# VectorE and ScalarE keep the written order of far-apart instructions in the RWKV recurrence of a hybrid DiT on one core

## The chip, the core and the metric

One core of a Trainium2 chip runs the whole forward pass in one launch. The metric is the device time of one execution in microseconds (us).

## The reference

The computation is a four-layer diffusion transformer on 256 latent and 256 context tokens, 1024 wide, in float32. The layers' mixers are, in this order, grouped-query attention with axial positions, neighbourhood attention on a 4 x 64 grid, a bidirectional RWKV-7 recurrence, and grouped-query attention again. Each layer adds a squared-ReLU MLP with 4096 hidden columns. The change lies in the third layer, whose core in the reference is a scan over tokens, run in both directions, for 16 heads of 64 columns:

```python
def step(s, inp):
    r_t, w_t, k_t, v_t, a_t, b_t = inp
    sa = jnp.einsum('nbhij,nbhj->nbhi', s, a_t)
    s = s * w_t[..., None, :] + sa[..., None] * b_t[..., None, :] + v_t[..., None] * k_t[..., None, :]
    return s, (jnp.einsum('nbhij,nbhj->nbhi', s, r_t) if emit else None)
```

## The kernel before

**Products.** Every weight is loaded in pieces of 128 x 1024 (`wr`) and split in two: ScalarE writes the high part `wh`, VectorE the remainder `wl` (class `Stream`, L259). A product is three TensorE matmuls: `wh`, `wl`, `wh` (L430 to L432; L470 to L472, tile `vps`, for the values of the RWKV layer, whose results are copied to `rV` at L1079, by VectorE and ScalarE in turn).

**The recurrence.** It is computed for pairs of heads, c = 0 to 7, each in blocks of 64 tokens. For one pair there are four kinds of work:
- `prep(c)` (L1099): gate products `wps` on TensorE with sigmoids `sg` and `ag` on ScalarE; the normed key (`ksq` on ScalarE, its sum over a head `kss` on TensorE, logarithm and exponential on ScalarE, `nkk`); the decays (a scan and `cc` on VectorE, two exponentials on ScalarE); the products `AR` and `BK`; a triangle `TT` from `tps`; a small triangular solve on GpSimd between two DRAM round trips, which ends in the load of `S` (L1234).
- `inverses(c)` (L1239): the transpose `R` of `S` on VectorE (L1250), `pa` and `pb` on TensorE with `cw` and `M` on VectorE, then `xd` on VectorE and four copies `Xt<-M` on ScalarE, `pv` and `px` on TensorE.
- `core(c)`, the chain (L1311): eight steps n, one after the other. A step's `zps` (TensorE) is copied to `z` (ScalarE), `ups` (TensorE) to `u` (ScalarE), then `sps` (TensorE) is scaled to the state `s` (VectorE), which the next step's `zps` needs. Masked products `nps` to `nmo` (VectorE), transposes `bkt` (copied by ScalarE) and the outputs `yps` stand beside it. 
- `post(c)` (L1414): group norm and gate of the outputs (`gm`, `bo`, `vT`, `gv`).

**What sets the order.** All these pieces are put in one list `todo` of (place, function). The place is counted in pairs: the chain of pair c has the places c to c + 1 in 46 or so equal steps, its `inverses` c - .65 to c - .1, its `prep` c - 2.4 to c - .9, its `post` c + 1 to c + 1.6. The list is sorted and the functions are called in that order (L1520); this is "the written order". It is not the order in which an engine executes: at build time a scheduler chooses, for each engine, among the instructions that are ready by its own cost model. It is bound by data and by order edges between two instructions of one engine, which set the order but give no semaphore. The class `InOrder` (L170) wraps an engine and can add such edges; before, it wraps ScalarE alone and is used only between `hold(True)` and `hold(False)`, outside the recurrence. An instruction that waits holds up those behind it in its engine's list, as the trace shows it where VectorE waits for `S`. Since ScalarE's calls pass through `InOrder`, all of its instructions have the line L180.

Of the kernel before, what the change touches and what calls it, by code (L numbers as in the profile page):

```python
# [169 lines left out]
class InOrder:  # L170


    def __init__(self, tc, engine):
        self.tc, self.engine, self.held, self.last = tc, engine, False, None

    def __getattr__(self, name):
        f = getattr(self.engine, name)

        def call(*args, **kw):
            x = f(*args, **kw)  # L180
            if self.held and getattr(x, "ins", None) is not None:
                if self.last is not None:
                    self.tc.add_manual_dep(x.ins, self.last, mybir.DependencyInfo(
                        mybir.DependencyClass.NoSync, mybir.DependencyReason.DATA), reason="order")
                self.last = x.ins.name
            return x
        return call

    def hold(self, on):
        self.held, self.last = on, None  # L190


@with_exitstack
def dit_kernel(ctx: ExitStack, tc: tile.TileContext, places, t_in, out, layers=DEPTH):
    nc = tc.nc
    pe, dve, pool, sp = nc.tensor, nc.vector, nc.gpsimd, nc.sync
    act = InOrder(tc, nc.scalar)

    one = ctx.enter_context(tc.tile_pool(name="one", bufs=1))
    k4p = ctx.enter_context(tc.tile_pool(name="k4", bufs=36))  # L200
# [11 lines left out]
    def pair(name, dt=F32):  # L212
        return k4(name, dt).rearrange("p (a t) -> p a t", a=2)

    def tmp(n, name):
        return t2p.tile([128, 520], F32, tag="t2", name=name)[:, 0:n]
# [4 lines left out]
    def bank(p, n, name):  # L221
        return p.tile([128, 512], F32, tag="b", name=name)[:, 0:n]
# [14 lines left out]
    def C(name, which="one"):  # L237
        o, shape = places[which][name]
        v = cs[which][:, o:o + int(np.prod(shape))]
        if len(shape) == 2:  # L240
            v = v.rearrange("p (a b) -> p a b", a=shape[0])
        elif len(shape) == 3:
            v = v.rearrange("p (a b c) -> p a b c", a=shape[0], b=shape[1])
        return v
# [178 lines left out]
    def split(dst, src, a, b, eng=dve):  # L423
        act.copy(out=dst[:, 0, a:b], in_=src)
        eng.tensor_tensor(out=dst[:, 1, a:b], in0=src, in1=dst[:, 0, a:b].bitcast(F32), op=ALU.subtract)  # L425
# [108 lines left out]
    def affine(dst, src, ca, cb, eng=None):  # L534
        (eng or dve).tensor_scalar(out=dst, in0=src, scalar1=ca, scalar2=cb, op0=ALU.mult, op1=ALU.add)
# [384 lines left out]
    def rwkv(i, hx, gate, nrm, begun, ends):  # L920
# [11 lines left out]
        def behind(x, others):  # L932
            for y in others:
                tc.add_manual_dep(x.ins, y.ins.name, mybir.DependencyInfo(
                    mybir.DependencyClass.NoSync, mybir.DependencyReason.DATA), reason="table set")

        def log(**kw):
            x = act.activation(**kw)
            if tables["set"] is not None:
                behind(x, [tables["set"]])  # L940
            tables["logs"].append(x)
# [113 lines left out]
        def keys(c):  # L1055
            def go():
                if c == 9:
                    W.depth = 1
                keep(c, 1, gemm(W.next("rw_wk", 0, "T", 0, c), m, ALL))
                if c == 7:  # L1060
                    made[4](PM)
            return go
# [351 lines left out]
        def post(c):  # L1414
            q = st[c]
            hold = {}

            def mean():
                y = tmp(512, "y")
                act.copy(out=y, in_=q["y"])  # L1420
                ps = bank(ps_s, 512, "gm")
                pe.matmul(ps, lhsT=ones64, rhs=y, start=True, stop=True)
                dve.scalar_tensor_tensor(out=y, in0=ps, scalar=-1.0 / 64, in1=y, op0=ALU.mult, op1=ALU.add)
                sq = tmp(512, "ysq")
                act.activation(out=sq, in_=y, func=AF.Square)
                hold["y"], hold["sq"] = y, sq

            def bonus():
                ps = bank(ps_s, 512, "bo")
                pe.matmul(ps, lhsT=ones64, rhs=q["rkd"], start=True, stop=True)  # L1430
                bo = q["rkd"]
                act.copy(out=bo, in_=ps)
                pt = bank(ps_s, 512, "vT")
                for blk in range(8):
                    for e in range(2):
                        pe.matmul(pt[half[e], blk * 64:blk * 64 + 64], lhsT=V[blk // 2][half[e], blk % 2, c], rhs=ident[half[e], half[e]], start=True, stop=True)
                dve.tensor_tensor(out=bo, in0=pt, in1=bo, op=ALU.mult)
                hold["bo"] = bo

            def var():  # L1440
                ps = bank(ps_s, 512, "gv")
                pe.matmul(ps, lhsT=ones64, rhs=hold["sq"], start=True, stop=True)
                r = hold["sq"]
                log(out=r, in_=ps, func=AF.Ln, bias=epg, scale=1.0 / 64)
                log(out=r, in_=r, func=AF.Exp, scale=-0.5)

            def normed():
                y = hold["y"]
                dve.tensor_tensor(out=y, in0=y, in1=hold["sq"], op=ALU.mult)
                affine(y, y, C("lnx_g", "rw")[:, c:c + 1], C("lnx_b", "rw")[:, c:c + 1])  # L1450

            def gated():
                ps = bank(ps_s, 512, "g")
                g2 = sml.tile([128, 128], F32, tag="g2", bufs=1, name="g2")
                sp.dma_start(out=g2, in_=t_in["rws"][c, :, 2])
                pe.matmul(ps, lhsT=g2, rhs=sig, start=True, stop=True)
                y = hold["y"]
                dve.tensor_tensor(out=y, in0=y, in1=hold["bo"], op=ALU.add)
                dve.tensor_tensor(out=y, in0=y, in1=ps, op=ALU.mult)

            def parts():
                o[c] = pair("o", F32R)
                split(o[c], hold["y"], 0, 512)
            return [mean, bonus, var, normed, gated, parts]
# [5 lines left out]
        def over(todo, a, b):  # L1470

            n = len(todo)
            return [(a + max(b - a, 0) * x / max(n - 1, 1), f) for x, f in enumerate(todo)]

        def weave(main, *side):

            for _, f in sorted(over(main, 0, 1) + [p for x in side for p in x], key=lambda p: p[0]):
                f()
# [19 lines left out]
        todo = over([keys(c) for c in range(8)], -2.6, -1.5)  # L1498
# [18 lines left out]
            todo += over([step(k) for k in range(9)], c - 2.4, c - 1.5)  # L1517
            todo += over([step(k) for k in range(9, 13)], c - 1.4, c - .9)
        todo.append((7., last_weights))
        for _, f in sorted(todo, key=lambda p: p[0]):  # L1520
            f()
        weave(begins, over(post(7), 0, .9))
        state["x"] = [pair("x") for _ in range(4)]
        for j in range(4):
# [127 lines left out]
    for i in range(layers):  # L1652
# [10 lines left out]
        def mid():  # L1663
            mod_to(i, 5)
            cols["e"] = Ends(nrm, i, 0, scales(i, 1, ln(0)))
            return cols["e"]

        streams = (gqa, natten, rwkv)[i % 3](i, get_h, gate, nrm, begun, mid)
        begun = cols["e"]
        nrm2 = Norm()  # L1670
# [37 lines left out]
def build(arrays, places, **kw):  # L1708
    import concourse.bacc as bacc

    nc = bacc.Bacc("TRN2", target_bir_lowering=False, num_devices=1)
    t_in = {n: nc.dram_tensor(f"in_{n}_dram", a.shape, F32, kind="ExternalInput").ap() for n, a in arrays.items()}
    out = nc.dram_tensor("out_0_dram", (128, 8, 256), F32, kind="ExternalOutput").ap()
    with tile.TileContext(nc) as tc:
        dit_kernel(tc, places, t_in, out, **kw)
    return nc
# [10 lines left out]
```

## Time and profile before

| | us |
|---|---|
| three runs | 2596.41, 2596.42, 2589.53 (median 2596.41) |
| the profiled execution, its own time | 2597.49 |
| its span, first to last instruction | 2595.7 |
| TensorE (PE) busy in it | 2469.1 (95%) |
| VectorE (DVE) busy | 1670.3 (64%) |
| ScalarE (ACT) busy | 1183.6 (46%) |
| GpSimd (POOL) busy | 267.7 (10%) |

The recurrence lies between about 1400 and 1850 us of the span. A row of the timeline gives start, duration, engine, line, operation, output and inputs, shapes and count, and in brackets how long the engine was idle before it and what ended that. A row of the waits gives the instruction that waited, what it waited for, the total in us, the number of times and the longest. A row of the windows gives the stretch, its length, the busy time of each engine, the clock that TensorE was granted as a share of its full 2.4 GHz, and the load of the DMA engines.

### The profile page before, as it was taken

The numbers are of one execution on the slowest core, as the hardware profiler recorded it, in microseconds if no ns is written. First come the engines' busy times: TensorE is split into PE (matmuls) and PEld (weight loads), VectorE is DVE, ScalarE is ACT, GpSimd is POOL, SyncE is SP. The second block draws the span as 40 slices with busy tenths as digits, with TensorE's granted clock in tenths as the row PEclk, the third lists the DMA queues.
The fourth block names the chain that finished last, engine by engine and source line by source line (L and its number), as shares of the span: only waits on it lengthen the run. The fifth ranks groups of instructions, "written<-read, shape, count | busy, mean of one in ns | idle before, by whom it ended". The sixth has DMA issues, their size and how long they took to land. (4 is left out here: it accounts for less than half of the span.)

```text
span 2595.7 us, 53219 instructions
## 1 busy us (share of the span) xinstructions
PE 2469.1 (95%) x22353; PEld 2096.9 (81%) x22353; DVE 1670.3 (64%) x3055; ACT 1183.6 (46%) x2214; POOL 267.7 (10%) x406
## 2 busy tenths in 40 slices
PE   8999999999999999999789799899989999999998
PEld 5778888889767888888767677778888888888997
DVE  3557677775566767787776565663658663766554
ACT  3555433244566543234455444544362343465644
POOL 0003000002000300000302112111030000221000
PEclk9999999999999999999899899999999999999998
DMA  8532556642111245664122311210336654223562
GB/s 324 170 124 66 180 192 191 208 147 94 59 60 58 82 144 182 202 210 162 67 95 83 78 28 32 41 23 12 140 95 215 208 188 126 82 66 106 179 188 89
DMA packets 158416, 324.14 MB, mean 125 GB/s; under 512 B 77392, under 2 KB 80992, under 8 KB 158176
## 3 DMA queue, kind: packets, MB, share of 16 engines
q1 hardware_dynamic: 158176, 320.73, 39.1%
q8 instruction: 176, 2.88, 0.5%
q14 instruction: 64, 0.52, 0.1%
HBM read 310.71 MB, written 9.97 MB: 124 GB/s over the span
## 5 line engine op out<-in xcount | busy, mean ns | idle before, releaser
L430 PE MATMUL mm<-h,wh 128*128 128x512 f32 (+1 forms) x1472 | 515.8, 353 | 19.1 <-ACT wh L180 10.4
L432 PE MATMUL mm<-h,wl 128*128 128x512 f32 (+1 forms) x1472 | 514.5, 350 | 4.3 <-DVE wl L280 4.0
L431 PE MATMUL mm<-h,wh 128*128 128x512 f32 (+1 forms) x1472 | 513.3, 349 | 2.6 <-DVE h L425 2.5
L180 ACT CAST wh<-wr 128x1024 fp32r<-128x1024 f32 x363 | 373.7, 1049 | 272.1 <-DVE wl L280 96.7
L280 DVE TENSOR_TENSOR wl<-wr,wh 128x1024 fp32r<-128x1024 f32 x340 | 426.5, 1261 | 93.6 <-ACT wh L180 72.0
L430 PE MATMUL mm<-f,wh 128*128 128x512 f32 (+1 forms) x1168 | 397.9, 341 | 0.0
L431 PE MATMUL mm<-f,wh 128*128 128x512 f32 (+1 forms) x1168 | 396.8, 340 | 0.0
L432 PE MATMUL mm<-f,wl 128*128 128x512 f32 (+1 forms) x1168 | 396.7, 340 | 0.0
L430 PEld LDWEIGHTS mm<-h,wh 128*128 128x128 f32 x1472 | 281.2, 192 | 63.9 <-ACT wh L180 12.5
L432 PEld LDWEIGHTS mm<-h,wl 128*128 128x128 f32 x1472 | 282.3, 192 | 42.7 <-DVE wl L280 6.9
L431 PEld LDWEIGHTS mm<-h,wh 128*128 128x128 f32 x1472 | 282.4, 192 | 39.3 <-DVE h L425 5.4
L431 PEld LDWEIGHTS mm<-f,wh 128*128 128x128 f32 x1168 | 221.6, 190 | 24.7
L430 PEld LDWEIGHTS mm<-f,wh 128*128 128x128 f32 x1168 | 221.6, 190 | 24.5
L432 PEld LDWEIGHTS mm<-f,wl 128*128 128x128 f32 x1168 | 221.6, 190 | 24.1
L180 ACT ACTIVATE relu<-mm 128x512 f32<-128x512 f32 (+1 forms) x146 | 72.5, 497 | 368.1 <-PE mm L432 368.1
L425 DVE TENSOR_TENSOR f<-sqr,f 128x512 fp32r<-128x512 f32 (+1 forms) x146 | 87.3, 601 | 229.4 <-ACT f L180 229.1
L483 DVE SCALAR_TENSOR_TENSOR x<-mm,gate,x 128x256 f32<-128x256 f32 x280 | 127.1, 480 | 142.8 <-PE mm L432 142.5
L280 POOL TENSOR_TENSOR wl<-wr,wh 128x1024 fp32r<-128x1024 f32 x23 | 60.8, 2645 | 1407.9 <-ACT wh L180 1400.4
L387 DVE SCALAR_TENSOR_TENSOR mwt<-mwt,srow 128x1024 f32<-128x1024 f32 x144 | 175.8, 1221 | 9.4 <-DMA mwt<-in_mwr_dram 8.0
L387 DVE SCALAR_TENSOR_TENSOR mpr<-mwt,srow 128x1024 f32<-128x1024 f32 x112 | 136.7, 1221 | 0.5
L430 PE MATMUL mm<-o,wh 128*128 128x256 f32 (+1 forms) x400 | 120.7, 303 | 0.3 <-ACT o L180 0.2
L432 PE MATMUL mm<-o,wl 128*128 128x256 f32 (+1 forms) x400 | 119.4, 299 | 0.3 <-DVE wl L280 0.2
(275 smaller groups left out, 4416.9 us busy)
## 6 DMA issues: line engine op xcount, KB each, us to landing
wr<-in_gw_dram SPq DMA_DIRECT2D x363, 512.0 KB, 3.7
mwt<-in_mwr_dram SPq DMA_DIRECT2D x144, 512.0 KB, 4.3
mwt<-in_mw_dram SPq DMA_DIRECT2D x48, 512.0 KB, 5.6
srow<-srow_d SPq DMA_DIRECT2D x6, 512.0 KB, 3.9
nab<-in_nab_dram SPq DMA_DIRECT2D x8, 384.0 KB, 3.3
rk<-rk_d SPq DMA_DIRECT2D x6, 512.0 KB, 4.7
rk_d<-rkp SPq DMA_DIRECT2D x10, 256.0 KB, 2.1
x<-in_xt_dram SPq DMA_DIRECT2D x4, 512.0 KB, 10.2
```

Of the source, the lines that this page charges most:

```text
L180: x = f(*args, **kw)
L280: self.lo[self.done % len(self.lo)].tensor_tensor(out=lo, in0=t, in1=hi.bitcast(F32), op=ALU.subtract)
L387: dve.scalar_tensor_tensor(out=to, in0=t, scalar=1.0, in1=rw_["s"][cnd], op0=ALU.mult, op1=ALU.mult, accum_out=m[:, cnd, r * 8 + c:r * 8 + ...
L425: eng.tensor_tensor(out=dst[:, 1, a:b], in0=src, in1=dst[:, 0, a:b].bitcast(F32), op=ALU.subtract)
L430: pe.matmul(ps, lhsT=st, rhs=hl[:, 0, a:b], start=first, stop=False)
L431: pe.matmul(ps, lhsT=st, rhs=hl[:, 1, a:b], start=False, stop=False)
L432: pe.matmul(ps, lhsT=wl[:, c * 128:(c + 1) * 128], rhs=hl[:, 0, a:b], start=False, stop=last)
L483: dve.scalar_tensor_tensor(out=xc(c)[:, a:b], in0=ps[:, a - base:b - base], scalar=gate[:, cnd, c:c + 1], in1=xc(c)[:, a:b], op0=ALU.mult, ...
```

## The change

`InOrder` gets a second mode, `within(reach)`, and VectorE is wrapped too. While the sorted list of the recurrence is called, each new instruction of VectorE or ScalarE gets an order edge to every earlier one of its engine whose place is lower by 0.1 or more (edges to instructions more than 0.3 back follow through those between). Two instructions of one engine that lie 0.1 of a pair apart can thus no longer be swapped by the scheduler; closer ones can. No instruction, transfer or buffer is added or taken away.

```diff
--- before.py
+++ after.py
@@ -170,31 +170,47 @@
 class InOrder:
 
 
+
     def __init__(self, tc, engine):
         self.tc, self.engine, self.held, self.last = tc, engine, False, None
+        self.reach, self.place, self.past = None, 0.0, []
+
+    def behind(self, x, name):
+        self.tc.add_manual_dep(x.ins, name, mybir.DependencyInfo(
+            mybir.DependencyClass.NoSync, mybir.DependencyReason.DATA), reason="order")
 
     def __getattr__(self, name):
         f = getattr(self.engine, name)
 
         def call(*args, **kw):
             x = f(*args, **kw)
-            if self.held and getattr(x, "ins", None) is not None:
+            if getattr(x, "ins", None) is None:
+                return x
+            if self.held:
                 if self.last is not None:
-                    self.tc.add_manual_dep(x.ins, self.last, mybir.DependencyInfo(
-                        mybir.DependencyClass.NoSync, mybir.DependencyReason.DATA), reason="order")
+                    self.behind(x, self.last)
                 self.last = x.ins.name
+            elif self.reach is not None:
+                for p, y in self.past:
+                    if p <= self.place - self.reach:
+                        self.behind(x, y)
+                self.past = [(p, y) for p, y in self.past if p > self.place - 3 * self.reach]
+                self.past.append((self.place, x.ins.name))
             return x
         return call
 
     def hold(self, on):
         self.held, self.last = on, None
+
+    def within(self, reach):
+        self.reach, self.past = reach, []
 
 
 @with_exitstack
 def dit_kernel(ctx: ExitStack, tc: tile.TileContext, places, t_in, out, layers=DEPTH):
     nc = tc.nc
-    pe, dve, pool, sp = nc.tensor, nc.vector, nc.gpsimd, nc.sync
-    act = InOrder(tc, nc.scalar)
+    pe, pool, sp = nc.tensor, nc.gpsimd, nc.sync
+    act, dve = InOrder(tc, nc.scalar), InOrder(tc, nc.vector)
 
     one = ctx.enter_context(tc.tile_pool(name="one", bufs=1))
     k4p = ctx.enter_context(tc.tile_pool(name="k4", bufs=36))
@@ -1517,8 +1533,14 @@
             todo += over([step(k) for k in range(9)], c - 2.4, c - 1.5)
             todo += over([step(k) for k in range(9, 13)], c - 1.4, c - .9)
         todo.append((7., last_weights))
-        for _, f in sorted(todo, key=lambda p: p[0]):
+
+        for eng in (act, dve):
+            eng.within(0.1)
+        for place, f in sorted(todo, key=lambda p: p[0]):
+            act.place = dve.place = place
             f()
+        for eng in (act, dve):
+            eng.within(None)
         weave(begins, over(post(7), 0, .9))
         state["x"] = [pair("x") for _ in range(4)]
         for j in range(4):
```

TensorE, GpSimd and SyncE get no edges of their own, but the scheduler's choices for them follow. In the row lists that the two kernels give, 208 of VectorE's 2801 instructions stand elsewhere, 104 of ScalarE's 2104, 686 of TensorE's 16807, 5 of SyncE's 735 and none of GpSimd's; all lie in the recurrence. In the changed kernel VectorE's instructions have the helper's line L186 too.

Three places. The first is ScalarE in the second half of a pair's chain, beside the `inverses` of the next pair (`Xt`, `v1`) and the start of the `prep` of the third one on (`sg`, `ag`, `ksq`); the same pattern stands in five pairs, c = 0 to 4. `z_15209`, `u_15227` and `bkt_15266` are the chain's copies. Before:

```order
L180 COPY z_15209<-zps_15200 128x128
L180 COPY u_15227<-ups_15222 128x128
L180 COPY bkt_15266<-bkt_15257 128x256
L180 ACT_TABLE_LOAD
L180 ACTIVATE sg_15142<-wps_15140,cs_rw_11519 128x8x64
L180 ACTIVATE sg_15146<-wps_15144,cs_rw_11519 128x8x64
L180 ACTIVATE ag_15150<-wps_15148,cs_rw_11519 128x512
L180 ACTIVATE ag_15153<-wps_15151,cs_rw_11519 128x512
L180 ACT_TABLE_LOAD
L180 COPY Xt_12313<-M_15065 32x16x32 x4
L180 ACTIVATE ksq_15229<-rk_14605,cs_rw_11519 128x512
```

And now:

```order
L186 COPY z_15209<-zps_15200 128x128
L186 ACT_TABLE_LOAD
L186 ACTIVATE sg_15142<-wps_15140,cs_rw_11519 128x8x64
L186 ACTIVATE sg_15146<-wps_15144,cs_rw_11519 128x8x64
L186 ACTIVATE ag_15150<-wps_15148,cs_rw_11519 128x512
L186 ACTIVATE ag_15153<-wps_15151,cs_rw_11519 128x512
L186 ACT_TABLE_LOAD
L186 COPY Xt_12313<-M_15065 32x16x32 x4
L186 COPY u_15227<-ups_15222 128x128
L186 ACTIVATE ksq_15229<-rk_14605,cs_rw_11519 128x512
L186 COPY v1_15238<-pv1_15239 128x128
L186 COPY bkt_15266<-bkt_15257 128x256
```

The chain's `u` stood ahead of the sigmoids and the copies `Xt<-M`; now it stands behind them, and the chain's `bkt` behind `ksq` and `v1`.

The second is VectorE at the start of the recurrence, around the transpose `R` of pair 0 (`S` comes by a DMA, `rV` are the value copies, `wl` the weights' remainders). Before:

```order
L1143 TENSOR_TENSOR cc_12877<-sg_12749 128x520
L1143 TENSOR_TENSOR cc_12941<-sg_12753 128x520
L1079 COPY rV_12766<-vps_12795 64x128 x2
L1250 STREAM_TRANSPOSE R_13055<-S_12738 128x512
L1079 COPY rV_12767<-vps_12795 64x128 x2
L1173 TENSOR_TENSOR fcol_13384<-sg_12749,cc_12877 128x3
L1173 TENSOR_TENSOR fcol_13384<-sg_12749,cc_12877 128x1
L1173 TENSOR_TENSOR fcol_13384<-sg_12749,cc_12877 128x3
L1173 TENSOR_TENSOR fcol_13384<-sg_12753,cc_12941 128x7
L1079 COPY rV_12768<-vps_12881 64x128 x2
L1079 COPY rV_12769<-vps_12881 64x128 x2
```

And now, the rows that end with the same transpose (`ag_12395` is of pair 0's `prep`, `AR`, `BK` and `TT` of pair 1's):

```order
L186 TENSOR_TENSOR ag_12395<-ag_12395,ag_12398 128x512
L186 TENSOR_TENSOR wl_12959<-wr_12800,wh_12958 128x1024
L186 SCALAR_TENSOR_TENSOR ag_12395<-ag_12395,cs_rw_11519,rk_11585 128x512
L186 TENSOR_TENSOR wl_12989<-wr_12830,wh_12988 128x1024
L186 TENSOR_TENSOR AR_13026<-nkk_12871,sg_12753 128x8x64
L186 COPY rV_12766<-vps_12957 64x128 x2
L186 COPY rV_12767<-vps_12957 64x128 x2
L186 SCALAR_TENSOR_TENSOR BK_13027<-nkk_12871,ag_12760 128x512
L186 TENSOR_TENSOR BK_13027<-BK_13027,cc_12941 128x512
L186 TENSOR_TENSOR TT_13032<-tps_13033,cs_rw_11519 128x512
L186 STREAM_TRANSPOSE R_13055<-S_12738 128x512
L186 COPY rV_12768<-vps_13057 64x128 x2
```

The transpose stood behind the first two `rV` copies and ahead of the others; now it comes some 25 instructions later, behind both `cc`, the products `AR` and `BK`, two `wl` and a `TT`.

The third is VectorE at the start of pair 0's chain, whose first `nmo` is `nmo_13571`. Before:

```order
L1079 COPY rV_12768<-vps_13469 64x128 x2
L1079 COPY rV_12769<-vps_13469 64x128 x2
L1332 TENSOR_TENSOR nmo_13571<-nps_13572,cs_rw_11519 128x384
L1275 TENSOR_TENSOR M_13280<-pb_13247,S_12738 128x256
L1275 TENSOR_TENSOR M_13280<-pb_13349,R_13055 128x256
L1119 MEMSET sg_13392 128x8
```

And now:

```order
L186 TENSOR_SCALAR ksq_13415<-kss_13417 128x512
L186 TENSOR_TENSOR BK_12946<-ag_12757,cc_12877 128x512
L186 SCALAR_TENSOR_TENSOR nkk_13422<-rk_12955,nkk_c_11525,ksq_13415 128x512
L186 SCALAR_TENSOR_TENSOR sg_13392<-resets_12306,sg_13392 128x520
L186 COPY rV_12768<-vps_13469 64x128
L186 TENSOR_TENSOR cc_13465<-sg_13392 128x520
L186 COPY rV_12768<-vps_13469 64x128
L186 COPY rV_12769<-vps_13469 64x128 x2
L186 TENSOR_TENSOR AR_13026<-rk_11638,sg_12753 128x8x64
L186 TENSOR_TENSOR fcol_13384<-sg_12753,cc_12941 128x7
L186 SCALAR_TENSOR_TENSOR sg_13396<-resets_12306,sg_13396 128x520
L186 TENSOR_TENSOR nmo_13571<-nps_13572,cs_rw_11519 128x384
```

The chain's `nmo` stood ahead of both `M`; now pair 1's `ksq`, `nkk`, its scans and `cc` and the last value copies are ahead of it.

## Rows read from the trace of the kernel before

**Rows 1.** The page: busy time of the engines, and the group of the high-part casts.

```profile
PE 2469.1 (95%) x22353; PEld 2096.9 (81%) x22353; DVE 1670.3 (64%) x3055; ACT 1183.6 (46%) x2214; POOL 267.7 (10%) x406
...
L180 ACT CAST wh<-wr 128x1024 fp32r<-128x1024 f32 x363 | 373.7, 1049 | 272.1 <-DVE wl L280 96.7
```

**Rows 2.** The windows from one pair's kss to the next; the clock is the column after POOL.

```profile
1579.93:1626.49 46.56, 42.54 (x1218) 34.48 (x1218) 29.86 (x63) 24.23 (x55) 10.49 (x32) 1.00 0.21 37
1626.49:1674.59 48.10, 43.71 (x1219) 35.11 (x1219) 29.89 (x63) 24.25 (x56) 10.41 (x32) 0.96 0.19 34
1674.59:1721.26 46.67, 42.69 (x1218) 34.56 (x1218) 29.98 (x63) 24.23 (x55) 10.78 (x34) 1.00 0.18 33
```

**Rows 3.** TensorE's waits from 1525 to 1750 us, five pairs: total, times, longest.

```profile
PE kss L1129 <- ACT ksq L180: 6.8, 5, 1.5
...
PE pv L1294 <- DVE xd L1281: 2.4, 5, 1.2
PE ups L1363 <- ACT z L180: 2.4, 5, 0.5
...
PE nps L1329 <- DVE nmo L1332: 1.6, 4, 0.5
PE zps L1355 <- DVE s L1384: 1.2, 5, 0.3
```

**Rows 4.** The timeline of ScalarE from 1568 to 1585 us, in one pair.

```profile
1569.11 0.27 ACT L180 COPY z<-zps 128x128 f32<-128x128 f32 x1 [1.26 <-PE zps L1355]
1570.01 0.27 ACT L180 COPY u<-ups 128x128 f32<-128x128 f32 x1 [0.64 <-PE ups L1363]
...
1571.62 1.28 ACT L180 ACT_TABLE_LOAD   x1
1572.91 1.26 ACT L180 ACTIVATE sg<-wps,cs_rw 128x512 f32<-128x512 f32 x2
...
1576.63 2.50 ACT L180 COPY Xt<-M 32x512 f32<-32x512 f32 x4
```

**Rows 5.** The timeline of TensorE in the same pair.

```profile
1569.51 0.40 PE L1363 MATMUL ups<-z,Xt 64*64 64x64 f32 x8
...
1572.25 1.13 PE L1114 MATMUL wps<-lora,wa 64*128 64x512 f32 x4
...
1576.38 0.45 PE L1374 MATMUL sps<-rV,bkt 64*64 64x64 f32 x8
1576.66 0.40 PE L1377 MATMUL sps<-u,bkt 64*64 64x64 f32 x8
```

**Rows 6.** All waits from 1425 to 1445 us, where the first pair's R is made.

```profile
DVE R L1250 <- DMA S<-rr: 8.3, 1, 8.3
...
PE pa L1259 <- DVE R L1250: 4.4, 1, 4.4
...
PE vps L470 <- ACT wh L180: 3.7, 1, 3.7
```

**Rows 7.** SyncE's queue from 1428 us, and the tile wr's issue-to-landing time.

```profile
1431.75 1.74 SPq L270 DMA_DIRECT2D wr<-in_gw_dram  x2
...
DMA to landing us min/median/max: 4.8/4.9/6.4
```

**Rows 8.** The timeline of VectorE from 1440 and from 1475 us.

```profile
1440.13 2.36 DVE L280 TENSOR_TENSOR wl<-wr,wh 128x1024 fp32r<-128x1024 f32 x2
...
1475.30 2.43 DVE L1140 TENSOR_TENSOR_SCAN sg<-resets,sg 128x520 f32<-128x520 f32 x2
...
1487.89 0.75 DVE L1134 SCALAR_TENSOR_TENSOR nkk<-rk,nkk_c,ksq 128x512 f32<-128x512 f32 x1 [1.91 <-ACT ksq L180]
```

**Rows 9.** TensorE from 1472 us, and short windows with the granted clock.

```profile
1472.71 0.33 PE L1329 MATMUL nps<-AR,BK 64*64 64x64 f32 x4 [2.47 <-ACT rV L180]
...
1473.00:1476.00 3.00, 2.34 (x36) 1.82 (x34) 1.96 (x6) 2.22 (x3) 2.52 (x7) 0.52 0.02 5
...
1626.70:1630.00 3.30, 3.30 (x32) 1.80 (x33) 0.69 (x1) 0.87 (x4) 0.00 (x0) 0.51 0.22 22
```

## The prediction

> **What bounds the kernel now.** I read the page first: TensorE is busy 95% of the span, VectorE 64%, ScalarE 46% [rows 1]. The change can only move what TensorE waits for, so the question in each stretch is which engine TensorE waits for, and for how long. All moved instructions lie in the recurrence, so I read windows there. From one pair's `kss` to the next it takes 46.56, 48.10 and 46.67 us, and TensorE is busy for 42.5 to 43.7 of it [rows 2]: the pair is close to TensorE's bound, with some 4 us of waits. The view of waits then tells which: over five pairs `kss` waits 6.8 us for ScalarE's `ksq` (1.36 a pair), `pv` 2.4 for VectorE's `xd`, `ups` 2.4 for `z`, `nps` 1.6 for `nmo`, `zps` 1.2 for `s` [rows 3]. The chain's own copy `u` is not among the large ones: ScalarE makes it at 1570.01, ahead of a long block, table load to `Xt`, that lasts from 1571.62 to 1579.13 [rows 4]. At the start of the recurrence one place stands out: VectorE is idle for 8.3 us in front of `R`, because `S` has not landed, and TensorE waits 4.4 us there and then 3.7 us for a `wh` [rows 6].
>
> **The change, part by part.** Nothing is added or removed; every term is an order.
>
> *ScalarE in the middle of a pair, five times.* Before, `u` is copied and then the block runs. Now the block goes first. I work out when `u` comes. The first `sg` began 0.66 us after its `wps` (1572.25 to 1572.91, [rows 4, 5]). In the new order of TensorE `wps` follows `ups` and four matmuls of `yps`; eight records, which are four matmuls of the code, take about 0.28 us (`sps` 1576.38 to 1576.66 [rows 5]), so `wps` starts near 1569.51 + 0.5 = 1570.0, `sg` near 1570.7. From `sg` to the end of `Xt` took 6.2 us [rows 4]; so `Xt` ends near 1576.9, and `u`, 0.27 us long, is there at 1577.2. What TensorE still has ahead of the first matmul that needs `u`: `ups` and four of `yps` (0.5), `wps` (1.1), eight of `bkt` (0.5), sixteen of `nps` (1.2) and half of `pv` (0.4), 3.7 us by the same prices, so it runs dry at 1573.2. The dry spell is **4.0 us**. In exchange `ksq` comes earlier and `kss` goes behind `sps` in TensorE's order, so what is late next is no longer `ksq`: the waits of `kss`, `pv` and `nps` go, 1.36 + 0.48 + 0.32 = 2.16 us a pair, and since VectorE and ScalarE get ahead during the spell I let those of `ups` and `zps` go too, 0.48 + 0.24. Net 4.0 - 2.9 = +1.1 us a pair, **+5.6 us** for five. Bounds: -2.9 if other work covers the whole spell, +5.5 if TensorE has nothing to do while ScalarE does block and copy (1571.62 to 1579.13 and 0.27, 7.7 us) and only the 2.16 go. I take a value between, as the cover of 3.7 us is counted.
>
> *The clock.* In the pair from 1626.49 TensorE was granted half its clock (1.2 instead of 2.4 GHz) for 3.3 us from 1626.70, right after a `kss` wait [rows 9]; that pair took 48.10 us, the two beside it 46.62 on average, so such a stretch costs about 1.5 us [rows 2]. Of the waits for `kss`, 1.5 us at most [rows 3], one brought it; after the 2.47 us wait at 1472.71 the clock was 0.52 between 1473 and 1476 [rows 9]. A dry spell of 4.0 us is longer than that one, so I expect one such stretch in each of the five pairs, where there is one now: 4 x 1.5 = **+5.9 us**. Bounds: -1.5 (none) and two in every pair, +13.5.
>
> The Trainium skill speaks of this in "TensorE: Matmul & The Clock Gate", section "A second HAM failure mode: psum-queue depth-cycling": a TensorE that idles briefly and often between groups of matmuls swings between the two clocks, and loses by each return. By that rule the short waits of before, too, should have cost the clock in every pair; the trace shows it in one of three [rows 2], so I count it by the length of the wait. For a spell as long as 4 us the rule would have it at least once in every pair; carried on to the waits that remain, it is the third rival.
>
> *ScalarE's table loads.* The block holds two, and the one in the row takes 1.28 us, with `sg` starting 0.01 us after its end [rows 4]. "ScalarE: Activation LUTs", section "What ACT_TABLE_LOAD costs", in the Trainium skill adds a drain of about 1.38 us to each load; by that `u` would come 2.8 us later still and the five pairs would lose some 14 us more. The row shows no such drain behind the load, and the sum goes by the row.
>
> *VectorE at `R`, once.* `R` moves behind some 25 instructions, which fill the 8.3 us of idle time. What is late next is the weights: the `wr` were issued at 1431.75 and land 4.9 us later, at 1436.65 [rows 7]; a cast of 1.05 [rows 1] and a `wl` of 1.18 (two in 2.36 [rows 8]) follow, so TensorE's value products can go on near 1438.9. Before, the first `wl` was done at 1440.13 + 1.18 = 1441.3 [rows 8]. That is **-2.4 us**. Bounds: 0, if those casts and `wl` queue behind something else, and -8.1, both waits gone [rows 6].
>
> *VectorE at the first `nmo`, once.* Ahead of it now stand pair 1's `ksq` and `nkk` with the wait for ScalarE between them (1.91), `nkk` itself (0.75), two scans (2.43 [rows 8]) and three more products that I put at 0.7 each by `nkk`: 7.2 us that pair 0's chain starts later. TensorE still has value products to do then, the order puts some 40 beside it; I take **+3.0 us**, between 0 (all covered) and 7.2 (nothing).
>
> *The rest.* SyncE's five moved loads pass only the loads of `rk` and stores near them; their transfers are hidden behind the waits above, and their price if that cover is gone is one landing, 4.9 us [rows 7]. At nothing: the last three pairs' order is nearly the same.
>
> Sum: 5.6 + 5.9 - 2.4 + 3.0 = +12.1 us on the profiled execution's 2597.5, or 2609.6. That execution lies 1.1 us above the median 2596.4, so the forecast for the median is **2608.5 us**. A difference of less than 0.3% (7.8 us) cannot be told from none.
>
> **The rivals.**
> - *The spell only takes the place of the old waits.* TensorE loses 1.1 us a pair but not the clock: 2608.5 - 5.9 = 2602.6 us, within 0.3%. For it: two of the three pairs kept the clock whole behind their `kss` wait [rows 2]. Against: the spell is more than twice as long as those.
> - *Faster: ScalarE's block is the true bound of the pair.* If TensorE's work covers the lateness of `u`, only the earlier `ksq` counts: 5 x 2.16 = 10.8 us go; with the +0.6 of the start, 2596.4 - 10.2 = 2586.2 us. The point from which it decides: TensorE must have some 7.7 us of work between `ups` and the first matmul on `u`. For it: `kss` is the largest wait of the pair [rows 3]. Against: I count 3.7 us there.
> - *Much slower: the clock falls twice in each pair*, once behind the spell and once behind the next wait: 2608.5 + 13.5 - 5.9 = 2616.1 us. For it: the low clock makes `u`'s successors late in turn. Against: the remaining waits are under 0.5 us [rows 3].
>
> **How the numbers follow.** I give the forecast 0.45, the first rival 0.30, the faster one 0.15, the much slower one 0.10. The forecast's own range is 2603 to 2614. The range of 8 in 10 leaves out most of the faster case and the upper half of the slowest: 2588 to 2617. Faster by over 0.3% needs less than 2588.6: 0.14. Slower by over 0.3% needs more than 2604.2: most of the forecast, the slowest case, and a small part of the first rival, 0.53. Within: 0.33.
>
> **What would show it.** In the changed profile's waits `sps` (or `yps`) should wait for ScalarE's `u`, near 4 us, five times, and `kss` hardly at all; the windows from `kss` to `kss` should be 47.5 to 49.5 us with a clock of 0.96 or so in each. VectorE's idle time before `R` should be gone and TensorE's wait there end with a `wh` or `wl`; the first `nmo` should follow a scan. I am wrong if the wait for `u` is under 2 us, if the clock stays at 1.00 in the pairs, or if the start gains or loses more than 5 us.

## The result and the profile after

The changed kernel takes 2627.07 us (median of 4 runs, 2623.72 to 2627.55) against 2596.41 us; the ratio is 1.0108, with a 95% interval of [1.0087, 1.0129]. It is slower, as forecast, but by some 28 us where 12 were forecast, and it lies above the range (2588 to 2617), above the slowest rival too (2616.1). All ratios, here and below, are to the kernel before, run again beside the kernel in question.

The windows from `kss` to `kss` in the profile after, to be read against [rows 2]; the number after POOL's column is the clock:

```profile
1540.30:1591.50 51.20, 44.87 (x1218) 36.20 (x1218) 30.25 (x63) 24.86 (x55) 8.69 (x32) 0.90 0.18 32
1591.50:1644.50 53.00, 44.99 (x1219) 36.32 (x1219) 30.26 (x63) 24.95 (x56) 8.62 (x32) 0.89 0.17 32
1644.50:1697.40 52.90, 44.11 (x1218) 35.10 (x1218) 30.25 (x63) 24.74 (x55) 8.78 (x32) 0.92 0.17 32
1697.40:1751.10 53.70, 44.72 (x1218) 35.80 (x1218) 30.16 (x63) 24.81 (x55) 8.74 (x32) 0.91 0.16 29
```

A pair, from one `kss` to the next, now takes 51 to 54 us instead of 46.6 to 48.1, and the clock is near 0.9 in every one. TensorE's waits over the same five pairs, 1525 to 1790 us, answer to [rows 3]:

```profile
PE sps L1390 <- ACT u L186: 16.7, 5, 3.4
PE kss L1145 <- ACT ksq L186: 13.5, 5, 3.8
PE ups L1379 <- ACT z L186: 3.1, 5, 0.9
```

The first row is the forecast's: `sps` waits for the late `u`, five times, 3.3 us each. The second is not: `kss`, whose wait was to go, waits twice as long as before. The timeline of ScalarE in one pair of the profile after says for what:

```profile
1584.59 1.28 ACT L186 ACT_TABLE_LOAD   x1
1585.89 2.50 ACT L186 COPY Xt<-M 32x512 f32<-32x512 f32 x4
1588.39 0.27 ACT L186 COPY u<-ups 128x128 f32<-128x128 f32 x1
1590.78 0.72 ACT L186 ACTIVATE ksq<-rk,cs_rw 128x512 f32<-128x512 f32 x1 [2.12 <-DMA rr<-lane]
```

`ksq` squares `rk` and has nothing to do with `lane`, the tile of GpSimd's triangular solve, nor with its store to DRAM. What it waits for must be the buffer (the runs below with other buffers bear this out). Both tiles come from one pool, t2 (the helper `tmp`, 18 buffers, L201 before), and in the new order `ksq` is given the one that `lane` held; it may write only when the store has read it. ScalarE's waits from 1525 to 1790 us and VectorE's from 1400 to 1460 us show the same releaser in both places:

```profile
ACT ksq L186 <- DMA rr<-lane: 15.5, 5, 3.9
```

```profile
DVE nkk L186 <- DMA rr<-lane: 7.2, 1, 7.2
```

At the start of the recurrence `nkk` has that buffer. The change took VectorE's 8.3 us in front of `R` away [rows 6] and put 7.2 us in front of `nkk`: one wait for the solve's end in exchange for another, some 6 us earlier. TensorE's waits there, which answer to the 4.4 and 3.7 us of [rows 6]:

```profile
PE tps L1216 <- ACT ag L186: 11.5, 1, 11.5
```

Marks in the two profiles put the loss together: `gm`, the first product of the group norm that follows a pair's chain. That of the first pair starts at 1553.2 instead of 1543.4 us (+9.8), that of the fifth at 1763.5 instead of 1731.6 (+31.9), that of the last pair at 1877.0 instead of 1841.3 (+35.7). So 10 us are lost by the start and the first pair, 22 in the next four, 4 in the last three; behind the recurrence, 5.6 us come back, to the 30.1 us between the two spans. That last part I did not trace; the stretch from the last mark to the end, where the order is unchanged, takes between 749 and 757 us in the fourteen profiles, so 5.6 us there need no cause in the change.

### The profile page after: what moved, and what is told of

The parts are those of the page before. It is cut to its first block, busy times and chain, and to the rows that moved or that the text cites. A ratio compares the mean times of both kernels' runs of the same rounds, so it can differ in the third digit from the quotient of the medians.

```text
span 2625.8 us, 53214 instructions
## 1 busy us (share of the span) xinstructions
PE 2473.9 (94%) x22353; PEld 2099.8 (80%) x22353; DVE 1672.7 (64%) x3055; ACT 1187.0 (45%) x2214; POOL 256.1 (10%) x406
## 5 line engine op out<-in xcount | busy, mean ns | idle before, releaser
L186 ACT CAST wh<-wr 128x1024 fp32r<-128x1024 f32 x363 | 373.7, 1048 | 270.0 <-DVE wl L186 96.7
L186 DVE TENSOR_TENSOR wl<-wr,wh 128x1024 fp32r<-128x1024 f32 x340 | 426.5, 1261 | 102.5 <-ACT wh L186 83.9
L186 ACT ACTIVATE relu<-mm 128x512 f32<-128x512 f32 (+1 forms) x146 | 72.5, 497 | 368.1 <-PE mm L448 368.1
L186 DVE TENSOR_TENSOR f<-sqr,f 128x512 fp32r<-128x512 f32 (+1 forms) x146 | 87.3, 601 | 229.4 <-ACT f L186 229.1
L186 DVE SCALAR_TENSOR_TENSOR x<-mm,gate,x 128x256 f32<-128x256 f32 x280 | 127.1, 479 | 143.5 <-PE mm L448 143.0
L186 DVE SCALAR_TENSOR_TENSOR mwt<-mwt,srow 128x1024 f32<-128x1024 f32 x144 | 175.8, 1221 | 8.6 <-DMA mwt<-in_mwr_dram 7.2
L186 DVE SCALAR_TENSOR_TENSOR mpr<-mwt,srow 128x1024 f32<-128x1024 f32 x112 | 136.7, 1220 | 0.5
```

## The experiments

**20 buffers, the order untouched.** Theories: the loss beyond the forecast is the waits for `lane`'s buffer, or it is the late `u` and its clock. Two more buffers change no place in any engine's list, only who waits for whose release.

```diff
-    t2p = ctx.enter_context(tc.tile_pool(name="t2", bufs=18))
+    t2p = ctx.enter_context(tc.tile_pool(name="t2", bufs=20))
```

> The changed kernel with 20 instead of 18 buffers of the pool t2; the order of instructions is the same on every engine, row for row, only the waits for a buffer's release differ: ksq in the pairs and nkk at the start no longer take the buffer of the triangular solve (lane), whose store they waited for. Theory 'buffers' (the loss beyond the forecast is those waits): kss no longer waits 2.7 us a pair, nkk not 7.2 us at the start; about 15 to 20 us come back, 2607 to 2612 us, the forecast. Theory 'order' (the late u alone with the clock it costs makes the loss): 2620 to 2627 us.

Measured: 2605.83 us, ratio 1.0039 [1.0026, 1.0052]. Against the changed kernel's 1.0108 that is 0.7%, or 18 us, for two buffers. TensorE's waits from 1525 to 1790 us and the windows of three pairs of this run:

```profile
PE sps L1390 <- ACT u L186: 16.8, 5, 3.4
...
```

```profile
1579.30:1627.10 47.80, 43.05 (x1220) 34.70 (x1219) 30.22 (x64) 24.97 (x56) 8.62 (x32) 0.96 0.18 34
1627.10:1675.20 48.10, 43.44 (x1219) 34.69 (x1219) 30.11 (x64) 24.78 (x56) 8.63 (x32) 0.96 0.21 36
1675.20:1724.30 49.10, 44.36 (x1220) 35.39 (x1219) 30.11 (x64) 25.32 (x57) 8.63 (x32) 0.95 0.16 30
```

The wait for `u` is the same, that of `kss` is gone from the list, a pair takes 48 to 49 us and the clock is 0.96 or 0.95: within what the forecast had said of the pair. At the start TensorE waits 5.6 us where the changed kernel waits 11.5. The time lies a little below the range of the first theory and far below that of the second: this decides for the buffers.

**Is it `lane`'s buffer or the size of the pool?**

```diff
-                lane = tmp(512, "lane")
+                lane = sml.tile([128, 512], F32, tag="lane", bufs=2, name="lane")
```

> The changed kernel with 18 buffers in t2, but the triangular solve's tile lane in two buffers of its own; the order of the instructions of TensorE, VectorE, ScalarE and SyncE is the same, row for row. Theory 'lane's buffer' (ksq and nkk wait for the store of lane): as with 20 buffers, 2602 to 2609 us, no wait of ksq in the pairs for a DMA. Theory 'size of the pool' (20 buffers helped in many places): 2615 us or more.

Measured: 2606.94 us, 1.0033 [1.0020, 1.0046], and no wait of `kss` among the largest. The pool is as large as in the changed kernel and the gain is nearly the same, so its size is not what helped. That it is `lane`'s buffer the releaser in the trace says too.

**Control: the kernel before with 20 buffers.**

```diff
-    t2p = ctx.enter_context(tc.tile_pool(name="t2", bufs=18))
+    t2p = ctx.enter_context(tc.tile_pool(name="t2", bufs=20))
```

> Control: the kernel before with 20 buffers in t2; the order is the same on every engine. All theories: the same time as before within 3 us (2593 to 2600 us), since no wait for a buffer ends last there; if it is faster by more, the larger pool helps by itself and the first run's gain has to be read less that.

Measured: 2595.01 us, 0.9997 [0.9985, 1.0010]. The larger pool is worth nothing here, so the 18 us are the price of the new order's choice of buffers.

**How much of it at the start?** VectorE's edges alone, and only below place 0, so that the chains of all pairs have the free order; with 20 and with 18 buffers the order is the same.

```diff
-        for eng in (act, dve):
+        for eng in (dve,):
             eng.within(0.1)
         for place, f in sorted(todo, key=lambda p: p[0]):
+            if place >= 0.0:
+                for eng in (act, dve):
+                    eng.within(None)
```

> Edges on VectorE alone and only for places below 0, 20 buffers in t2: R behind the products as in the changed kernel, the first nmo and all pairs free. Theory 'the pairs lose, R gains': TensorE's wait at R is 5.6 us instead of 8.2, pairs of 46.9 us: 2588 to 2595 us, below before. Theory 'the start is even whatever VectorE does': 2594 to 2599 us.

> As the run with VectorE's edges below place 0, same order on every engine, but with 18 buffers: of the waits for lane's buffer only the one of nkk at the start is back, none in the pairs. Theory 'the start's wait is part of the loss': VectorE waits some 7 us at nkk, TensorE 11.5 instead of 5.8 before the next weights, 6 to 10 us slower than with 20 buffers: 2597 to 2601 us. Theory 'only the pairs' waits cost': within 3 us of the run with 20 buffers, 2588 to 2594 us.

Measured: 2590.88 us, 0.9970 [0.9959, 0.9982] with 20 buffers; 2593.45 us, 0.9990 [0.9978, 1.0002] with 18. TensorE's waits from 1400 to 1460 us with 20 buffers, and VectorE's there with 18:

```profile
PE vps L486 <- ACT wh L186: 5.8, 1, 5.8
```

```profile
DVE nkk L186 <- DMA rr<-lane: 7.3, 1, 7.3
```

With 18 buffers TensorE's wait there is 10.9 us. The difference of the two ratios is 0.2%, 5 us, as large as the difference of the waits (10.9 - 5.8 = 5.1), though the two intervals overlap a little, and in us the second run lies in the range of the second theory (2588 to 2594). The traces speak for the first: the first `gm` comes at 1542.8 us with 18 buffers and at 1538.1 with 20, 4.7 us earlier, and the next four pairs take the same (187.9 and 187.6 us). So of the 18 us about 5 are lost at the start and, by subtraction, 13 later, most of it in the pairs. With 20 buffers this version is faster than both kernels: it is the part of the change that pays. Over the kernel before the gain is 0.3%, which is the limit of what the prediction called distinguishable.

**The late `u`.** Here `u` gets no edge; 20 buffers.

```diff
-                    act.copy(out=hold["u"], in_=ps)
+                    nc.scalar.copy(out=hold["u"], in_=ps)
```

> As the run with 20 buffers, but the chain's copy u gets no order edge, so it stands ahead of ScalarE's block again. Theory 'late u': the 3.3 us waits of sps vanish, with them the half clock in the pairs, and about 12 us come back against the run with 20 buffers. Theory 'VectorE's order': the pairs gain under 4 us, since zps or nps then wait for VectorE.

Measured: 2606.96 us, 1.0040 [1.0027, 1.0053], no gain at all against 20 buffers alone (1.0039). The waits of TensorE say why:

```profile
PE kss L1145 <- ACT ksq L186: 12.1, 5, 2.6
```

`sps` waits no longer, but `kss` waits 2.4 us a pair for `ksq`, which stands behind the same block of ScalarE, and the clock falls at least as far: 0.87 to 0.96 in the four windows, 0.95 to 0.96 with 20 buffers alone. (The traced execution, 2615.04 us, was the slowest of this run's eight.) The time fits the second expectation, but not its reason: `zps` waits 0.8 us for VectorE in all five pairs together and `nps` not at all. The late `u` did not add its spell to the pair; it had taken the place of a wait for `ksq`, and both stand behind one block.

**One engine at a time.** Edges on ScalarE alone (18 buffers; `ksq` has a free one there), and on VectorE alone (20 buffers).

```diff
-        for eng in (act, dve):
-            eng.within(0.1)
+        act.within(0.1)
```

> The order edges on ScalarE alone; VectorE as before. u is late, ksq has a free buffer, R and nmo stand nearly as before. Theory 'late u': the waits of sps near 4 us in five pairs with a half clock, no loss at the start: 2604 to 2611 us. Theory 'buffers or VectorE': within 4 us of before, 2593 to 2601 us.

```diff
-        for eng in (act, dve):
-            eng.within(0.1)
+        dve.within(0.1)
```

> Edges on VectorE alone, 20 buffers in t2. Theory 'VectorE's order' (what is left of the loss, 10 us, comes from it, since the run with u freed gained nothing): 2602 to 2609 us, kss waits 2.4 us for ksq in each pair. Theory 'ScalarE's order': 2593 to 2599 us, pairs of 46.9 us as before.

Measured: 2600.19 us, 1.0021 [1.0010, 1.0033], and 2602.37 us, 1.0021 [1.0006, 1.0035]. The first lies in the range of its second theory (2593 to 2601), the second in that of its first (2602 to 2609). Each costs some 5 us, together (1.0039) 10. With ScalarE's edges alone `sps` waits 12.7 us in five pairs, with VectorE's alone `kss` waits 12.3. That the remaining 10 us divide evenly is not shown: with ScalarE's edges alone the pool has 18 buffers, and at the start VectorE's `cc` waits 6.7 us for the store of `lane`, so part of these 5 us can be that.

**Edges from place 0 on only,** with 20 buffers: the start as before.

```diff
-        for eng in (act, dve):
-            eng.within(0.1)
...
+            if place >= 0 and act.reach is None:
+                for eng in (act, dve):
+                    eng.within(0.1)
             act.place = dve.place = place
```

> Edges on both engines only from place 0 on, 20 buffers in t2: the start keeps the order of before. Theory 'the pairs' (the order costs 1.3 us a pair and as much in the tail, the start is even): 2602 to 2609 us. Theory 'the start': 2594 to 2599 us.

Measured: 2606.19 us, 1.0035 [1.0022, 1.0048]: within the interval of the run with edges from the beginning (1.0039). So the 10 us are lost from place 0 on; the edges of both engines ahead of it, with 20 buffers and with those behind it in force, neither gain nor lose anything clear of noise.

**Is ScalarE's block the bound of the pair?** The normed key goes ahead of the gate products, so `ksq` precedes the block; once on the best version, once on the kernel before with 20 buffers.

```diff
-            out.append(gate_products)
...
             out.append(unit_k)
+            out.append(gate_products)
```

> As the run with VectorE's edges below place 0 and 20 buffers, and in prep the normed key goes ahead of the gate products, so ksq stands ahead of ScalarE's block with the table loads. Theory 'ScalarE's block bounds the pair': the waits of kss (6.6 us in five pairs) vanish and 4 to 8 us come back: 2583 to 2588 us. Theory 'another wait takes their place': within 3 us, 2588 to 2594 us.

> The kernel before with 20 buffers and the normed key ahead of the gate products. Theory 'ScalarE's block bounds the pair': 4 to 8 us faster than before, 2588 to 2593 us. Theory 'another wait takes their place': within 3 us of before, 2593 to 2600 us.

Measured: 2600.15 us, 1.0016 [1.0005, 1.0027], and 2604.60 us, 1.0032 [1.0018, 1.0047]. A miss for both expectations: the wait of `kss` is gone, but both are slower than without the edit (0.9970 and 0.9997). The first run's waits, 1525 to 1790 us, and one of its pairs:

```profile
PE ups L1379 <- ACT z L186: 7.2, 6, 1.7
PE pv L1310 <- DVE sg L186: 3.1, 5, 1.4
```

```profile
1572.20:1621.10 48.90, 43.86 (x1219) 35.32 (x1219) 30.76 (x63) 25.03 (x55) 7.67 (x29) 0.97 0.19 34
```

Other waits have taken its place, of the chain for `z` (3.0 us without the edit) and of `pv` behind the scans `sg`. With them goes the clock: in this pair and the next two it is 0.93 to 0.97 and a pair takes 48.9 to 49.6 us, where the run without the edit keeps 1.00 and takes 46.1 to 47.3. The edit also moves the gate products, and with them the scans, to a later place; so it does not isolate the block, and whether the block bounds the pair stays open.

**A longer reach.** 0.3 of a pair, 18 buffers.

```diff
-            eng.within(0.1)
+            eng.within(0.3)
```

> The changed kernel with a reach of 0.3 instead of 0.1 of a pair, 18 buffers: u stands ahead of ScalarE's block again, and neither ksq nor nkk takes lane's buffer. Theory 'the loss is in those two': within 4 us of before, 2592 to 2601 us. Theory 'any edge costs': 2603 us or more.

Measured: 2591.93 us, 0.9990 [0.9976, 1.0003]. Not to be told from before, so edges as such need not cost anything. My reading of who gets `lane`'s buffer was half right: in the pairs only one `nkk` waits for it (3.2 us at 1630 us), and at the start now `cc` does, by VectorE's waits from 1400 to 1460 us:

```profile
DVE cc L186 <- DMA rr<-lane: 6.7, 1, 6.7
```

## Why the prediction failed

The direction was right, and so were the places; the size was not. The main reason is one missing term, the waits for `lane`'s buffer, 18 of the 28 us; of the rest some terms missed in both directions and partly cancelled.

- *"the waits of `kss`, `pv` and `nps` go"*: **this step failed.** Those of `pv` and `nps` did go (and that of `zps`; that of `ups` stayed, 3.1 us in five pairs). That of `kss` went from 6.8 to 13.5 us, since `ksq`, although next in ScalarE's list right behind `u`, waited 2.1 to 3.9 us for the store of `lane`. I costed the new order by data and by queue, and never asked whose buffer a moved instruction writes. With the waits for that buffer taken out, and nothing else, the kernel takes 2605.8 us, where 2608.5 had been forecast. That this is so near is in part luck, by the next points.
- *`u` late, the spell of 4.0 us*: 3.3 us measured, five times. As a cost by itself it was misread: with `u` freed, `kss` waits in its stead and the time stays. My reading is that the pair pays for the block of ScalarE ahead of both; no run isolates that.
- *The clock, +5.9 us, one stretch a pair*: in the run with 20 buffers the windows show 0.95 to 0.96, as one stretch a pair would. But clock and spell together were too dear: the three pairs shown of that run take 48.3 us on average, the three of before 47.1 [rows 2], 1.2 us more (0.6 of it idle, 0.6 busy) where 1.1 + 1.2 had been forecast, so some 6 us in five pairs instead of 11.5. In the changed kernel it is 0.89 to 0.92, since the second wait brings more. The windows of one pair of the changed kernel:

```profile
1588.50:1591.50 3.00, 1.33 (x18) 1.14 (x18) 0.58 (x2) 0.89 (x3) 0.00 (x0) 0.50 0.42 44
1591.50:1598.00 6.50, 6.45 (x98) 4.65 (x100) 4.22 (x6) 2.82 (x7) 0.00 (x0) 0.50 0.62 145
1598.00:1604.00 6.00, 5.76 (x188) 5.25 (x190) 5.43 (x12) 4.63 (x12) 0.00 (x0) 1.00 0.02 5
```

  The half clock (1.2 GHz) holds from the end of the wait for `u` through the one for `ksq` and for 6.5 us behind it, and TensorE is busy for almost all of those 6.5 us. That is near the third rival's mechanism, a second wait that costs the clock again; here the two stretches run into one. The argument against it, that the remaining waits are short, was wrong for `kss`. By the Trainium skill ("TensorE: Matmul & The Clock Gate", section "A second HAM failure mode: psum-queue depth-cycling") repeated idling between groups of matmuls brings such swings between the two clocks. This case agrees for nearly all waits above 2 us (an exception stands in the last section); those of 1.5 us did not always do it [rows 2, 3].
- *Two table loads of 1.28 us in the block* [rows 4]: 1.28 again, `Xt` 0.02 us behind the end of the second. The drain of "ScalarE: Activation LUTs" (section "What ACT_TABLE_LOAD costs") in the Trainium skill shows in no row here.
- *`R`, -2.4 us*: the idle time before `R` is gone, but the weights did not come next. `nkk` waited 7.2 us for the same solve. Behind it stood the scans, the `cc`, and on ScalarE their exponentials, ahead of the casts `wh`, which began at 1440.08 where I had put them at 1436.65. TensorE waited 11.5 us, where before it waited 4.4 + 3.7 = 8.1 [rows 6]. With 20 buffers it waits 5.6 us: 2.5 less than before, near the forecast's 2.4, but by luck. There it waits for `BK`, at `tps`, and not for a weight, and the casts `wh` begin at 1432.59, before the landing that I had counted on.
- *The first `nmo`, +3.0 us*: in the run with 20 buffers TensorE waits 3.7 us at `kss` and 6.1 at `nps` there, where before it waited 2.5 us at `nps`; the first `gm` starts at 1543.1 us, as before (1543.4). The start as a whole is even, forecast +0.6; what this term alone cost, no run shows.
- *The last three pairs, at nothing*: 113.5 us from the fifth `gm` to the last, 109.7 before, 110.9 with 20 buffers. So 1 us by the order and some 3 more by the buffers, on single executions.

The faster rival held that ScalarE's block bounds the pair. Its condition, that TensorE's work covers the lateness of `u`, did not come about: TensorE waits 3.3 us for `u` in each of five pairs. Placing `ksq` ahead of the block took the wait of `kss` away and was slower, so in that form an earlier `ksq` was not worth the 10.8 us that this rival gave it.

## What to carry to other kernels

An order of instructions also decides which buffer of a shared pool each tile gets, and with it who waits for whose last reader: before costing a reordering, list the new waits of the moved instructions, and look for a releaser that has nothing to do with their data. Two experiments settle such a wait without touching the order: one or two more buffers in the pool, and the suspected holder in buffers of its own. An order forced everywhere can hide a part that pays: here VectorE's edges at the start alone, with 20 buffers, take 0.3% off the kernel before, about as little as can be told from none.

## What was unexpected of the hardware

A wait of 2.1 to 2.6 us of TensorE in a busy stretch was mostly enough to halve its clock: with `u` freed, `kss` waits so long in five pairs and a stretch at 1.2 GHz follows each time; with VectorE's edges alone it follows four of five. The fifth, a wait of 2.25 us that ends at 1531.6 us, left the clock whole, so the length of the wait alone does not decide:

```profile
1531.60:1538.00 6.40, 6.27 (x165) 4.92 (x166) 3.66 (x7) 3.99 (x13) 0.00 (x0) 1.00 0.68 153
```

Two waits of 3.3 and 1.5 us in close succession left 9.5 us at half clock (1588.5 to 1598.0 in the changed kernel). And the store of one small tile, with its landing, holds a buffer for long: its two parts were issued from 1587.37 us on, and `ksq` could start at 1590.78, 3.4 us later.

```profile
1587.37 1.31 SPq L1248 DMA_DIRECT2D rr<-lane  x2
```
